# A decoder trunk on one core: the entry, the exit and the aftermath of a seven-product up projection

## The chip, the core and the metric

The kernel runs on one core of a Trainium2 chip. The core has five engines that matter here: TensorE (PE), which multiplies; VectorE (DVE); ScalarE (ACT); GpSimd (POOL); and SyncE (SP), which only issues DMAs. Each engine works through its own list of instructions in order and waits on semaphores. ACT issues DMAs as well, from within its own list. The metric is the device time of one execution in microseconds (us), as the median of several runs.

## The reference

Two groups of rows, a prompt of 1024 rows and 8 samples of 8 rows, go through two layers with the same weights; together they are T = 1088 columns of a transposed activation. Each layer is a token mixer, a gated feed-forward part and a gated addition:

```python
for i in range(DEPTH):
    j = i // N_MIXERS
    xn = rms_norm(h, g_mix[i])
    if i % N_MIXERS == 0:
        mix, s = short_conv_mixer(xn, st_a[j], a_w_in[j], a_conv[j], a_w_out[j])
    else:
        mix, s = conformer_conv_mixer(xn, st_b[j], ...)
    h = h + mix
    h = h + swiglu_ffn(rms_norm(h, g_ffn[i]), ffn_w_gu[i], ffn_w_down[i])
    gate = jax.nn.sigmoid(rms_norm(h, g_ple[i]) @ ple_w_gate[i])
    h = h + gate * (p[i] @ ple_w_proj[i])
return rms_norm(h, g_final), ...
```

D_MODEL is 1024 (KD = 8 tiles of 128) and D_FF is 2816 (KF = 22 tiles). Everything is float32. The change concerns layer 0 only: the end of its mixer, its up projection `x @ w_gu` with `silu(g) * u`, and its down projection.

## The kernel before, in words

**Precision.** Every float32 operand is cut into a high part, which PE takes in its faster float32 format, and a low part (the rest). A product is three matmuls: high by high, high by low, low by high. The high part of a weight (`whi`) is a copy on ACT. The low part (`wlo`) is a subtraction on POOL, or, for later weights, a load of a low part that was computed ahead of time and stored in DRAM.

**Staging.** Computing those low parts ahead of time is called staging (`stage`, line 245). 110 weight units of 512 KB are staged in 220 halves: load a half into `sraw`, copy its high part to `shi` on ACT, subtract on POOL, store the result (`dlo`). `stage()` is called after every block or product; the code keeps a running estimate of PE's time (`nc.tensor.at`, from the class `Paced`) and does one step whenever that estimate has advanced by `STAGE_EVERY`. In a step, ACT issues the store of the half that POOL has finished, copies the next half and issues the load of a new one. Before a pool of `sraw` buffers can be closed, `stage_with` (line 276) finishes all that is in flight, one half after the other.

**The mixer (`mixer_a`, line 520; 0 to about 440 us).** Its last step is eight items of four blocks each; a block is nine matmuls (three chunks of the 1088 columns, three partial products). The loop runs over `MIX_J` = 0, 4, 1, 5, 2, 6, 3, 7. After each item `mixer_end` (line 568) adds the PSUM result to h on DVE, writes h to DRAM (`hd`), adds the squares for the norm (`norm_stat`, also on DVE) and, after every second item, calls `operands(k)` (line 584) for the pair of row tiles k and k + 4. At its first item `at_end[0]` (`last_down`, line 1157) closes the staging's buffers, at its last item `at_end[1]` (`last_item`, line 1176) makes the first weights of the next stage ahead of the add.

**The seven-product stage (`ffn0_up`, line 631; about 420 to 906 us).** Each pair of gate and up weight tiles is multiplied as a 2 by 2 block product with seven instead of eight block multiplications. The seven products of a pair f are A11·B11, S2·T2, S3·T3, S1·T1, S4·B22, A12·B21 and A22·T4. The left factors are sums of quarter weights: `pair_fetch` loads a pair's raw weights on SP, `pair_sums` makes S1 to S4 on DVE, `pair_cell` cuts one of them into high and low parts in a ring of ten buffers. The right factors come from `operands`: B11, B21, B22 are halves of h times the gain, T1 to T4 are their differences. A product is 24 matmuls of 272 columns. `next_weights(m)` prepares pair f + 1 between the products of pair f. Within the first pair (f == 0) the sums of squares are reduced over the partitions by matmuls with a matrix of ones, and 1/sqrt is taken (`rms`, line 494): `rms[0]` cuts the sums into high and low parts, `rms[1]` does the matmuls and the root. At the end of each pair the activation is written to DRAM (`ad`). PSUM holds four buffers in this stage.

**The down projection (`ffn0_down`, line 695; from 932 us on).** h was given up for space and is loaded again from `hd`. The activations are loaded from `ad` into `ta`, cut into high (ACT) and low (DVE) parts, and multiplied in batches of `DOWN_0` = 3, 4, 4, 4, 4, 3. Each batch runs over the eight row tiles j; after each item DVE adds the PSUM result to h. The activations of the next batch are loaded and cut in the first items of this one. PSUM holds two buffers here. In the last batch, after its first item, `swap` (line 1217) does all staging that is left, closes the pools of the operands and opens those of the next stage; from then on each item is followed by two norm splits (`hna`, `hn`) on ACT and DVE.

**What sets the order.** The schedule is written by hand: the order of the calls is the order on each engine. SP's list holds the loads of weights, h and ta and the stores of h and ad; ACT's list holds the staging's DMAs.

Of the kernel before, what the change touches and what calls it, by code (L numbers as in the profile page):

```python
# [19 lines left out]
P = 128  # L20
# [42 lines left out]
DOWN_0 = [3, 4, 4, 4, 4, 3]  # L63
# [81 lines left out]
class Net:  # L145
# [3 lines left out]
    def __init__(self, ctx, tc, xT, wall, pT, sa, sb, vecs, yT, sa_p, sa_s, sb_p, sb_s):  # L149
# [16 lines left out]
        self.stage_slots, self.stage_at = None, 0.0  # L166
# [78 lines left out]
    def stage(self, flush=False):  # L245
# [23 lines left out]
        if self.to_stage and not flush:  # L269
            u, i = self.to_stage.popleft()  # L270
            raw = self.stage_slots[1]("sraw", F32)
            self.stage_slots.append(self.stage_slots.pop(1))
# [3 lines left out]
    def stage_with(self, slots):  # L276

        while self.stage_raw or self.staging:
            self.stage(True)
        self.stage_slots, self.stage_at = slots, self.nc.tensor.at  # L280

    def stage_tiles(self, pool, n):
        return [lambda name, dtype, i=i: pool.tile([P, WH], dtype, name=name, tag=f"s{i}", bufs=1) for i in range(n)]
# [236 lines left out]
    def mixer_a(self, y):  # L520
# [6 lines left out]
        def up(f):  # L527
# [6 lines left out]
            else:  # L534
                psc, psh = self.item(g, y), self.item(g, y)
            t = self.tmp(g)
# [31 lines left out]
    def mixer_end(self, i, ps):  # L568
# [15 lines left out]
    def operands(self, k):  # L584
# [14 lines left out]
        put("B21", hb[:, lo], gb)  # L599
        nc.scalar.activation(yb, hb, AF.Copy, scale=gb)  # L600
        nc.vector.tensor_tensor(ya[:, lo], ya[:, up], ya[:, lo], ALU.subtract)
        nc.vector.tensor_tensor(ya[:, up], yb[:, up], ya[:, up], ALU.subtract)
        put("T1", ya[:, lo])
        nc.vector.tensor_tensor(yb[:, up], yb[:, up], ya[:, lo], ALU.subtract)
        put("T2", yb[:, up])
        put("B22", hb[:, up], gb)
        put("T3", ya[:, up])
        nc.vector.tensor_tensor(yb[:, lo], yb[:, lo], yb[:, up], ALU.subtract)
# [853 lines left out]
```

## Time and profile before

| | us |
|---|---|
| runs before | 2595.93, 2598.44, 2743.23 |
| median | 2598.44 |
| profiled execution, its own time | 2593.68 |
| its span, first to last instruction | 2591.9 |
| PE busy | 2476.4 |
| DVE, ACT, POOL busy | 1403.2, 1001.4, 952.3 |

A profile row of the timeline gives the start, the length (us), the engine, the line, the operation with the names of what it writes and reads, its shape and its count; a bracket at the end gives the idle time of that engine just before and what ended it. All instructions of this kernel carry line 128, the helper that records them, so that rows are told apart by their tile names: `ps` is PSUM, `y` an operand of the seven products, `ya` and `yb` its sources, `w` and `ws` their weights and sums, `act` the down projection's operand, `hna` and `hn` the norm splits. A row of the waits gives the engine and what it writes, the engine and tile that it waited for, the total in us, the number of times and the longest. SPq and ACTq mark the issue of a DMA, not its transfer.

### The profile page before, as it was taken

The page shows a single profiled execution, that of the slowest core. Times are in us where ns is not written, and L with a number is a line of the kernel's source. Part 1 is how long each engine was busy: PE and PEld are TensorE (multiplying, and loading weights), DVE is VectorE, ACT ScalarE, POOL GpSimd, SP SyncE. Part 2 cuts the span into 40 slices and gives each one's busy share as a digit, 9 for nine tenths or more (in the row PEclk, how much of TensorE's full clock was granted, in tenths as well). Part 3 has the DMA queues.
Part 4 walks back from the last instruction along what each step waited for, and adds up shares of the span by engine and source line. Part 5 has one row for each costly group of instructions (what it writes and reads, how often), then busy time and mean ns, then how long its engine had stood idle before and what let it go on. Part 6 is the DMA issues. An engine that isn't in the chain of part 4 may idle for free.

```text
span 2591.9 us, 39114 instructions
## 1 busy us (share of the span) xinstructions
PE 2476.4 (96%) x15590; PEld 2283.1 (88%) x15590; DVE 1403.2 (54%) x1947; ACT 1001.4 (39%) x1377; POOL 952.3 (37%) x655
## 2 busy tenths in 40 slices
PE   9999987999999959995999999999999999999998
PEld 8898977999999949995789897888887899999997
DVE  5222238888888733333587776688865532222235
ACT  5222235433333323224554535444335542222235
POOL 3555551555555435554233433333333110000012
PEclk9999998999999979997999999999999999999999
DMA  4444442555555466554555475555555575454445
GB/s 139 138 154 157 141 140 97 181 188 193 189 185 191 153 244 213 199 197 138 181 195 197 167 190 177 188 186 189 188 188 193 186 259 202 167 163 163 164 163 198
DMA packets 183575, 462.71 MB, mean 179 GB/s; under 512 B 38368, under 2 KB 41824, under 8 KB 183392
## 3 DMA queue, kind: packets, MB, share of 16 engines
q1 hardware_dynamic: 118880, 342.60, 38.9%
q10 hardware_dynamic: 64512, 117.60, 14.1%
q8 instruction: 123, 2.02, 0.3%
q14 instruction: 60, 0.49, 0.1%
HBM read 375.65 MB, written 84.48 MB: 178 GB/s over the span
## 4 chain that ended last, share of the span: by engine, by line
PE 50%; DVE 2%; ACT 1%; DMA 1%; POOL 0%; issue 0%; ACTq 0%; DVEq 0%; POOLq 0%; SPq 0%
PE ps L128 50%; DMA dlo<-sraw 0%; POOL sraw L128 0%; DVE t L128 0%; DMA wlo<-dlo 0%; DVE acc L128 0%; DVE h L128 0%; ACT ua L128 0%; DVE hna L128 0%; DVE nt L128 0%; ACT cact L128 0%; ACT shi L128 0%; ACTq L128 0%; DMA sraw<-wall 0%; DVE nv L128 0%
## 5 line engine op out<-in xcount | busy, mean ns | idle before, releaser
L128 PE MATMUL ps<-hn,whi 128*128 128x288 f32 (+3 forms) x4416 | 915.1, 323 | 3.2 <-ACT whi L128 2.3
L128 PEld LDWEIGHTS ps<-hn,whi 128*128 128x128 f32 x4416 | 692.7, 189 | 58.5 <-ACT whi L128 2.5
L128 PE MATMUL ps<-act,whi 128*128 128x288 f32 (+1 forms) x2496 | 519.5, 332 | 74.5 <-DVE h L128 47.1
L128 PE MATMUL ps<-hn,wlo 128*128 128x288 f32 (+3 forms) x2208 | 562.8, 323 | 2.6 <-DMA wlo<-dlo 2.6
L128 PEld LDWEIGHTS ps<-act,whi 128*128 128x128 f32 x2496 | 392.9, 191 | 115.6 <-DVE h L128 37.2
L128 PE MATMUL ps<-y,w 128*128 128x272 f32 x3696 | 472.3, 290 | 11.6 <-ACT w L128 3.4
L128 PEld LDWEIGHTS ps<-y,w 128*128 128x128 f32 x3696 | 470.9, 190 | 13.1 <-ACT w L128 3.8
L128 POOL TENSOR_TENSOR sraw<-sraw,shi 128x512 fp32r<-128x512 f32 x220 | 318.6, 1448 | 359.8 <-issue 131.7
L128 PEld LDWEIGHTS ps<-hn,wlo 128*128 128x128 f32 x2208 | 364.8, 189 | 29.6 <-DMA wlo<-dlo 2.9
L128 ACT ACTIVATE whi<-wraw 128x1024 fp32r<-128x1024 f32 (+1 forms) x282 | 293.5, 1042 | 204.0 <-PE ps L128 158.5
L128 PE MATMUL ps<-act,wlo 128*128 128x288 f32 (+1 forms) x1248 | 306.8, 332 | 0.3 <-POOL wlo L128 0.3
L128 DVE TENSOR_TENSOR h<-ps,h 128x1088 f32<-128x1088 f32 (+2 forms) x200 | 184.7, 925 | 225.3 <-PE ps L128 225.0
L128 POOL TENSOR_TENSOR t<-t,r 128x512 f32<-128x512 f32 (+2 forms) x52 | 80.4, 1546 | 538.2 <-ACT t L128 493.1
L128 ACT ACTIVATE shi<-sraw 128x512 fp32r<-128x512 f32 x220 | 137.6, 625 | 300.6 <-POOL sraw L128 285.6
L128 DVE TENSOR_TENSOR t<-ps,t 128x544 f32<-128x544 f32 (+3 forms) x155 | 115.4, 746 | 255.4 <-PE ps L128 247.8
L128 PEld LDWEIGHTS ps<-act,wlo 128*128 128x128 f32 x1248 | 201.2, 191 | 19.6 <-POOL wlo L128 0.8
L128 ACT ACTIVATE t<-t 128x512 f32<-128x512 f32 (+5 forms) x107 | 76.6, 717 | 333.8 <-DVE t L128 333.7
L128 POOL TENSOR_TENSOR sqacc<-sqacc,sq 128x512 f32<-128x512 f32 (+4 forms) x69 | 97.7, 1416 | 261.8 <-ACT sq L128 261.5
L128 POOL TENSOR_TENSOR prod<-prod 128x512 f32<-128x512 f32 x96 | 124.2, 1303 | 180.7 <-ACT prod L128 180.6
L128 POOL TENSOR_TENSOR wlo<-wraw,whi 128x1024 fp32r<-128x1024 f32 (+1 forms) x54 | 136.1, 2524 | 138.2 <-ACT whi L128 132.3
L128 DVE TENSOR_TENSOR t<-ps,r 128x512 f32<-128x512 f32 (+3 forms) x116 | 78.9, 683 | 187.7 <-PE ps L128 186.9
L128 DVE SCALAR_TENSOR_TENSOR acc<-ub,vecs_sb,acc 128x512 f32<-128x512 f32 x184 | 137.6, 749 | 4.0 <-ACT acc L128 4.0
(154 smaller groups left out, 2419.6 us busy)
## 6 DMA issues: line engine op xcount, KB each, us to landing
wraw<-wall SPq DMA_DIRECT2D x322, 512.0 KB, 3.9
wlo<-dlo SPq DMA_DIRECT2D x226, 512.0 KB, 3.6
sraw<-wall ACTq DMA_DIRECT2D x220, 256.0 KB, 3.3
dlo<-sraw ACTq DMA_DIRECT2D x220, 256.0 KB, 2.5
ad<-t SPq DMA_DIRECT2D x22, 544.0 KB, 4.3
ta<-ad SPq DMA_DIRECT2D x22, 544.0 KB, 5.4
h<-xT SPq DMA_DIRECT2D x8, 544.0 KB, 6.8
hd<-h SPq DMA_DIRECT2D x8, 544.0 KB, 2.9
```

Source lines behind the costliest of these rows:

```text
L128: return f(out, *args, **kw)
```

## The change

- **Staging.** The buffers for `shi` and `sraw` are separate lists now (two and four in the mixer and in the down projection, one and four in the seven-product stage). A step is done every 3.9 instead of 4.4 counted us, from 30 instead of 50 on, with less catching up after a delay. A flag `stage_ends` stops the fetching of new halves while the steps go on. It is set in the mixer's last up item, at the start of the last pair of the seven-product stage, and in the fifth batch of the down projection at j = 5. `swap` does no staging any more and asserts that nothing is left to stage.
- **Operands in two parts.** `operands(k)` makes B11, B21 and the first difference, and leaves the rest (T2, T3, T1, B22, T4, in this order) to a function that the next `mixer_end` calls after its add of h. For the last pair it is called at once, ahead of the norm sum.
- **Norm sums.** In the first pair of the seven-product stage the cut of the sums moves behind the S2 product's add, and the matmuls with the ones matrix and the root move behind the S1 product.
- **Next weights.** For f > 0 each step of `next_weights` comes one product later.
- **The down projection's loads.** A function `early`, called in the last pair ahead of the S4 product, fetches the first two weight units, loads and cuts the first two activations and loads all eight tiles of h, in the order 3, 7, 1, 2, 4, 5, 0, 6. Before, this came after the last pair. The batches are 2, 4, 4, 4, 4, 4. Within the batches an activation is loaded from ACT's queue ahead of the item and cut after the item's add of h; before, SP's queue loaded it and it was cut at once, behind the add.

```diff
-DOWN_0 = [3, 4, 4, 4, 4, 3]
+DOWN_0 = [2, 4, 4, 4, 4, 4]
...
-        self.stage_at = max(self.stage_at + self.STAGE_EVERY, nc.tensor.at - 2 * self.STAGE_EVERY)
+        self.stage_at = max(self.stage_at + self.STAGE_EVERY, nc.tensor.at - self.STAGE_EVERY / 2)
         done, self.staging = self.staging, None
         nc.scalar.wait(nc.tensor)
-        ahead = len(self.stage_slots) - 3
+        his, raws = self.stage_slots
...
-        ready = len(self.stage_raw) == ahead or flush or not self.to_stage
-        if ready and self.stage_raw:
+        fetch = self.to_stage and not self.stage_ends
+        if self.stage_raw and (len(self.stage_raw) == len(raws) - 2 or not fetch):
             u, raw = self.stage_raw.popleft()
-            hi = self.stage_slots[0]("shi", F32R)
+            hi = his[0]("shi", F32R)
+            his.rotate(-1)
...
-        if self.to_stage and not flush:
+        if fetch:
...
                 psc, psh = self.item(g, y), self.item(g, y)
+                self.stage_ends = f == KD - 1
...
         self.add_h(g, j, ps)
+        if self.rest:
+            self.rest.pop()()
         self.hd[j] = self.pd.tile([P, T], F32, name=f"hd{j}")
         self.nc.sync.dma_start(self.hd[j], self.h[j])
         if i % 2:
             self.operands(j - KH)
+        if i == KD - 1:
+            self.rest.pop()()
         self.norm_stat(g, j, self.nc.vector)
...
+        nc.vector.tensor_tensor(ya[:, lo], ya[:, up], ya[:, lo], ALU.subtract)
         nc.scalar.activation(yb, hb, AF.Copy, scale=gb)
...
+        def rest():
+            nc.vector.tensor_tensor(ya[:, up], yb[:, up], ya[:, up], ALU.subtract)
+            nc.vector.tensor_tensor(yb[:, up], yb[:, up], ya[:, lo], ALU.subtract)
+            put("T2", yb[:, up])
+            put("T3", ya[:, up])
+            nc.vector.tensor_tensor(yb[:, lo], yb[:, lo], yb[:, up], ALU.subtract)
+            put("T1", ya[:, lo])
+            put("B22", hb[:, up], gb)
+            put("T4", yb[:, lo])
+
+        self.rest.append(rest)
...
-                if f == 0:
-                    m -= 2
+                m -= 1 if f else 2
...
             if f == 0:
-                rms[1]()
+                halves()
             next_weights(1)
             add(s[:, lo], go("S3", "T3"), t[:, up])
             next_weights(2)
             q = go("S1", "T1")
+            if f == 0:
+                factors()
             add(t[:, up], q, t[:, up])
             add(s[:, up], q, s[:, lo])
             next_weights(3)
+            if f == KF - 1:
+                early()
             add(t[:, up], go("S4", "B22"), t[:, up])
...
+    def act_load(self, queue):
+        f = len(self.acts)
+        low, high = (pool.tile([P, T], F32R, name="act", tag=tag, bufs=1) for pool, tag in self.places.popleft())
+        t = self.tmp(GJ, "ta")
+        queue.dma_start(t, self.ad[f])
+        self.acts.append((high, low))
+        return t
+
+    def act_split(self, f, t):
+        high, low = self.acts[f]
+        self.nc.scalar.activation(high, t, AF.Copy)
+        self.nc.vector.tensor_tensor(low, t, high.bitcast(F32), ALU.subtract)
...
             for j in range(KD):
-                self.add_h(g, j, self.item(g, acts[at:at + n]))
+                if not last and j < DOWN_0[b + 1]:
+                    loads.append((len(self.acts), self.act_load(nc.scalar)))
+                if b == len(DOWN_0) - 2 and j == KD - 3:
+                    self.stage_ends = True
+                self.add_h(g, j, self.item(g, self.acts[at:at + n]))
+                if loads:
+                    self.act_split(*loads.pop(0))
...
+        def early():
+
+            self.n_raw = self.n_prep = N_MIX + 2 * KF
+            self.blk = self.n_raw * KD
+            self.limit = len(self.order)
+            self.n_conv += 2
+            self.fetch_to(self.n_raw + self.RAW)
+            t = [self.act_load(nc.sync) for _ in range(DOWN_0[0])]
+            self.prep_to(self.n_raw - self.RAW + 1)
+            for f in range(DOWN_0[0]):
+                self.act_split(f, t[f])
+            for j in range(KD):
+                self.h[j] = ph.tile([P, T], F32, name=f"h{j}", tag=f"h{j}")
+            for j in 3, 7, 1, 2, 4, 5, 0, 6:
+                nc.sync.dma_start(self.h[j], self.hd[j])
...
         def swap():
-            for _ in range(len(self.to_stage)):
-                self.stage_at = 0.0
-                self.stage()
-            self.stage_with(None)
+            assert not self.to_stage
+            self.stage_with()
...
-    STAGE_EVERY = 4.4
-    STAGE_FROM = 50.0
+    STAGE_EVERY = 3.9
+    STAGE_FROM = 30.0
```

More of the change, by code (lines that the diff above doesn't have):

```diff
@@ L268, in stage, with stage_with, stage_tiles @@
             self.staging = u, raw
-        if self.to_stage and not flush:
+        if fetch:
             u, i = self.to_stage.popleft()
-            raw = self.stage_slots[1]("sraw", F32)
-            self.stage_slots.append(self.stage_slots.pop(1))
+            raw = raws[0]("sraw", F32)
+            raws.rotate(-1)
             nc.scalar.dma_start(raw, self.wall[u][:, i * WH:(i + 1) * WH])
             self.stage_raw.append(((u, i), raw))
-    def stage_with(self, slots):
+    def stage_with(self, his=None, raws=None):
+        self.stage_ends = True
         while self.stage_raw or self.staging:
             self.stage(True)
-        self.stage_slots, self.stage_at = slots, self.nc.tensor.at
-    def stage_tiles(self, pool, n):
-        return [lambda name, dtype, i=i: pool.tile([P, WH], dtype, name=name, tag=f"s{i}", bufs=1) for i in range(n)]
+        self.stage_slots, self.stage_at = his and (deque(his), deque(raws)), self.nc.tensor.at
+        self.stage_ends = False
+    def stage_tiles(self, pool, a, b):
+        return [lambda name, dtype, i=i: pool.tile([P, WH], dtype, name=name, tag=f"s{i}", bufs=1) for i in range(a, b)]
     ORDER = "A11", "S2", "S3", "S1", "S4", "A12", "A22"
@@ L635, in ffn0_up, with halves @@
         r = self.rg(g)
-        rms = [f for _, f in self.rms(g, 0, 0)]
+        self.parts = [self.pt.tile([P, T], F32R, name=n, tag="t") for n in ("sh", "sl")]
+        def halves():
+            nc.scalar.activation(self.parts[0], self.sqacc, AF.Copy)
+            nc.vector.tensor_tensor(self.parts[1], self.sqacc, self.parts[0].bitcast(F32), ALU.subtract)
+        (_, _), (_, factors) = self.rms(g, 0, 0)
         for f in range(KF):
             if f == 0:
-                rms[0]()
                 self.pair_fetch(1)
+            if f == KF - 1:
+                self.stage_ends = True
             t, s = self.tmp(g), self.tmp(g, "s")
@@ L1137, in run @@
         self.pu0 = pool("u0", c_u, bufs=2)
-        self.hd, self.ad, self.right = {}, {}, {}
-        self.stage_with(self.stage_tiles(pool("stage_m", c_st), 6))
+        self.hd, self.ad, self.right, self.rest = {}, {}, {}, []
+        p = pool("stage_m", c_st)
+        self.stage_with(self.stage_tiles(p, 0, 2), self.stage_tiles(p, 2, 6))
         self.stage_at = self.STAGE_FROM
@@ L1191, in run @@
         self.PSW = GS.width
-        self.stage_with(self.stage_tiles(pool("stage_u", c_st), 5))
-        self.ffn0_up()
-        self.stage_with(None)
+        p = pool("stage_u", c_st)
+        self.stage_with(self.stage_tiles(p, 0, 1), self.stage_tiles(p, 1, 5))
+        py, py2 = self.cells["T2", 0][0], self.cells["B11", 0][0]
+        places = [[(py2, f"z{2 * i}"), (py2, f"z{2 * i + 1}")] for i in range(3)]
+        places += [[(py, f"y{2 * i}"), (py, f"y{2 * i + 1}")] for i in range(5)]
+        self.places = deque(places[i % len(places)] for i in range(KF - DOWN_0[-1]))
+        self.acts = []
+        def early():
[12 more added lines that the diff above has]
+                nc.sync.dma_start(self.h[j], self.hd[j])
+        self.ffn0_up(early)
+        self.stage_with()
         c_st.close()
-        self.n_conv += 2
         c_x.close()
@@ L1226, in swap @@
             self.pYA = pool("y_a", c_ya, side="right", bufs=KD)
-        ya, yb = self.ffn0_down(places, swap)
+        ya, yb = self.ffn0_down(swap)
         c_x.close()
```

53 lines of the change are left out of this document (12 added, 41 removed).

## The prediction, made before the changed kernel ran

> **What bounds the kernel now.** I read the page first, then the waits of the whole run, then TensorE (PE) alone by windows, then the timeline around each hole.
>
> ```profile
> span 2591.9 us, 39114 instructions
> PE 2476.4 (96%) x15590; PEld 2283.1 (88%) x15590; DVE 1403.2 (54%) x1947; ACT 1001.4 (39%) x1377; POOL 952.3 (37%) x655
> PE   9999987999999959995999999999999999999998
> ```
>
> PE sets the time: 115.5 us of the span are idle, and the slices show three holes in the first half (slices 7, 15 and 19). The waits name them:
>
> ```profile
> PE ps L128 <- DVE h L128: 47.1, 6, 27.2
> PE ps L128 <- ACT whi L128: 28.5, 2, 26.2
> ```
>
> They are the stage's entry (about 353 to 481 us), its exit (906 to 957) and the place where the down projection changes its pools (1180 to 1213). A hole costs more than its idle time; PE by windows (length, busy, granted clock):
>
> ```profile
> 353.30:481.00 127.70, 100.62 (x612) 0.87 0.33 114
> 402.70:407.30 4.60, 4.58 (x18) 0.63 0.38 148
> 932.30:935.90 3.60, 3.29 (x10) 0.50 0.13 11
> 951.90:956.60 4.70, 4.66 (x19) 0.64 0.32 74
> 1207.60:1213.00 5.40, 5.30 (x19) 0.54 0.15 42
> ```
>
> Behind each hole PE runs at half to two thirds of its clock: 1.7, 1.8, 1.7 and 2.5 us lost (length times the missing clock).
>
> **The pool change (third hole).**
>
> ```profile
> 1178.40:1204.30 25.90, 6.29 (x10) 12.62 (x10) 0.63 0.61 203
> 1171.61 1.29 DVE L128 TENSOR_TENSOR h<-ps,h 128x1088 f32<-128x1088 f32 x1 [3.16 <-PE ps L128]
> 1204.20 0.72 ACT L128 ACTIVATE hna<-h,vecs_sb 128x512 fp32r<-128x512 f32 x1 [1.80 <-POOL sraw L128]
> 1206.36 1.28 DVE L128 TENSOR_TENSOR h<-ps,h 128x1088 f32<-128x1088 f32 x1
> 1207.69 2.18 PE L128 MATMUL ps<-act,whi 128*128 128x288 f32 x6 [27.24 <-DVE h L128]
> 1214.45 1.16 PE L128 MATMUL ps<-act,whi 128*128 128x288 f32 x6
> 1215.95 1.16 PE L128 MATMUL ps<-act,whi 128*128 128x288 f32 x6
> ```
>
> The first row holds ACT's and POOL's work on shi: ten weight halves are still staged at 2.5 us each, one after the other, ahead of the hna copy on ACT. DVE waits for hna, the next add of h stands behind it, and PE has only two PSUM buffers. Cost: 27.24 + 2.5 = 29.7 us.
>
> The change empties this work earlier. A block of nine matmuls takes 1.50 us (last two rows), for which the pacing counts 1.39, so one half per 3.9 counted is one per 4.2 us. Until the mark (fifth batch, j = 5) there are about 300 us of the mixer (from counted 30 to its own mark near 341), 147 products of 3.02 us (444 us; 21.1 us for seven is in the exit's first row) and 132 blocks (198 us): 942 / 4.2 = 224 halves, and 220 are wanted. From the mark to the swap 16 blocks follow, 24 us, nearly six steps, for the three still in flight. So the swap finds nothing to flush. I take 28.5 of the 29.7; bounds 22 (three halves left) and 29.7. The faster staging lies beside PE: POOL is busy 37% and ACT 39%, and neither made PE wait in a steady stretch.
>
> **The exit (second hole).**
>
> ```profile
> 884.83 21.32 PE L128 MATMUL ps<-y,w 128*128 128x272 f32 x168
> 888.84 21.45 SPq L693 DMA_DIRECT2D ad<-t  x2
> 910.34 7.14 SPq L1206 DMA_DIRECT2D h<-hd  x8
> 932.34 2.18 PE L128 MATMUL ps<-act,whi 128*128 128x288 f32 x6 [26.19 <-ACT whi L128]
> 948.25 1.11 ACT L128 ACTIVATE act<-ta 128x1088 fp32r<-128x1088 f32 x1 [7.50 <-DMA ta<-ad]
> 951.94 1.26 PE L128 MATMUL ps<-act,whi 128*128 128x288 f32 x6 [3.91 <-DVE h L128]
> DMA to landing us min/median/max: 4.3/5.4/9.3
> ```
>
> Before, SP issues h, then ta, then the weights only after the last pair's store. Lost: 26.19 + 1.8, then 3.91 + 1.7, and 0.6 of small waits: 34.2 us.
>
> After, two weight units, two ta tiles and h go out within the last pair. Counting from the last pair's start (884.8), with landings of 4.5 to 5.5 us (last row): SP issues the store of pair 20 at 889 and is free, the raws land by 895, the ta tiles by 896 and 898.5 (the second waits for that store to give back its buffer), and the two splits (1.11 on ACT, on DVE as long as an add of h, 1.28 each) end at 901, while the S4 product ends at 899.9 (five of 3.02). They stand ahead of the S4 add on DVE; that add is 1 us late, which free PSUM buffers cover. SP's h loads queue behind the third raw (which waits for wlo) and, for h5, h0, h6, behind the products that last read those slots; h0 lands near 910, just when DVE gets to the first add. So PE restarts about 1 us after the last product.
>
> What is late next is the first batch. It has two activations now, so an item lasts 3 us, and in its first four items one activation each is loaded through **ACT's queue**: trigger, landing, copy, and only then the next trigger. With 4.5 us to land (minimum 4.3 for one alone) and 1.11 + 0.35, a step takes 6 us. DVE's subtract waits for it, and the next add of h stands behind the subtract, so with two PSUM buffers PE follows the 6 us steps: items 4, 5 and 6 wait 1.9, 2.9 and 2.8, and one slow restart adds 1.7. In the later batches an item lasts 6 us and the step hides. Left: 1 + 7.6 + 1.7 and about 1 for staging steps between, 11.3; gain **23 us**. Bounds: 13 (steps of 8.5 us: the median landing plus two staging copies) and 30 (all hidden but the restart).
>
> The Trainium skill (DMA: Bandwidth & Descriptors, the cost of one DMA) gives a fixed 2.0 us and bytes over 436 GB/s, an estimate of 3.3 us for these 557 KB; no load here landed in less than 4.3, and by the rule the batch would wait some 3 us less, 2528 in all.
>
> **The entry (first hole).**
>
> ```profile
> 365.44 1.29 DVE L128 TENSOR_TENSOR h<-ps,h 128x1088 f32<-128x1088 f32 x1 [4.79 <-PE ps L128]
> 373.76 0.78 DVE L128 SCALAR_TENSOR_TENSOR y<-h,vecs_sb,y 128x544 fp32r<-128x544 f32 x1 [7.04 <-ACT y L128]
> 386.91 2.15 PE L128 MATMUL ps<-act,whi 128*128 128x288 f32 x6 [9.35 <-DVE h L128]
> 389.15 1.28 DVE L128 TENSOR_TENSOR h<-ps,h 128x1088 f32<-128x1088 f32 x1
> 401.29 1.28 DVE L128 TENSOR_TENSOR h<-ps,h 128x1088 f32<-128x1088 f32 x1
> 402.72 1.43 PE L128 MATMUL ps<-act,whi 128*128 128x288 f32 x6 [2.22 <-DVE h L128]
> 404.96 1.28 DVE L128 TENSOR_TENSOR h<-ps,h 128x1088 f32<-128x1088 f32 x1
> 420.71 1.75 DVE L128 TENSOR_TENSOR ws<-wraw 128x512 f32<-128x512 f32 x1
> 428.05 1.28 DVE L128 TENSOR_TENSOR h<-ps,h 128x1088 f32<-128x1088 f32 x1
> 430.08 8.69 PE L128 MATMUL ps<-y,w 128*128 128x272 f32 x52 [0.81 <-DVE y L128]
> 444.47 28.90 PE L128 MATMUL ps<-y,w 128*128 128x272 f32 x216
> 473.21 0.69 DVE L128 TENSOR_TENSOR ws<-wraw 128x512 f32<-128x512 f32 x1 [6.17 <-DMA wraw<-wall]
> 476.65 23.56 PE L128 MATMUL ps<-y,w 128*128 128x272 f32 x185 [3.28 <-DVE t L128]
> ```
>
> A flush of staging on ACT holds the first operands back 7.04 us; from there DVE is the bound until 444. Two items cost it 15.8 us (389.15 to 404.96), PE 12. Without the flush the chain starts at 366.7. With the operands in two parts the second part goes to the even item, and T2, T3, T1 are copied back to back, so most of DVE's waits for ACT's copies go; I count 5.5 us for an odd and 8.6 for an even item (1.21 per add, 0.65 per half-width operation): 14.1. The even item of step 2 starts with PE at 371.4, so the chain reaches the pair-0 sums at 408.2 (420.71 before), the last add of h at 415.5 (7.3 us of sums and cells, as before) and the first operand B11 of the last k at 417.6 against 430.1: 12.5 us earlier.
>
> The norm sums now follow S1, so five products run on without them. They need PE 14.8 us with a slow start, the sums 1.5, and DVE's three reads come after the pair-1 sums, at 434.3; S4 starts at 434.9. Before it was 444.47 + 1.7 + two products, 452.2. PE's 3.28 wait for the pair-2 raws' sums comes again (raws at 459, adds at 462). Gain **16 us**. Bounds: 7 (the flush alone; also what is left if S4 had to wait for S1's own buffer through the whole 1/sqrt chain, which it does not if the buffer given back first goes out first), and 22 (no second wait).
>
> The Trainium skill (TensorE: Matmul & The Clock Gate, the two clock states) has the clock fall after a whole idle window of about 3.4 us. Here 2.22 us of waiting were enough for 0.63, but 16 us after a longer hole. By the rule the short waits of the first down batch would keep the clock and give 1.7 us back; by the row they do not.
>
> **Edits that I cost at nothing.** *The earlier end of fetching* in the mixer and in the last pair: three halves in flight need 12.6 us, and 12 blocks (18 us) or seven products (21 us) follow the mark. If that cover were gone, each half left would cost ACT 2.5 us, as in the third hole. *The second shi buffer* takes away a wait of ACT for POOL that no PE wait hung on. *The batches of 2 and 4 instead of 3 and 3* hold the same 176 blocks; the last batch's items grow from 4.5 to 6 us, above what ACT and DVE do in one (add, two copies, two subtracts). *The act loads on ACT* leave SP to the weights, which it held up before (a load at ACT's head waits for no weight buffer); in exchange ACT's weight copies stand behind a landing, up to 6 us late, under units of 12 us prepared two ahead.
>
> **The sum.** 28.5 + 23 + 16 = 67.5 us. The profiled execution took 2593.7 us around its 2591.9 us span, and would take 2526; the median of the runs is 2598.4, so I forecast **2531 us**.
>
> **Rivals.**
> *Load chain.* The first down batch goes at 9 us per step, since ACT's staging triggers wait for POOL behind wlo. For it: two wlo fall in that time. Against: staging restarts with two steps that only fetch. Four steps of 3 us more: 2543.
> *Entry stays DVE's.* Splitting saves no time on DVE, only the flush goes: 9 us less, 2540. For it: DVE's number of operations is the same. Against: 3 us of waits per two items.
> *Not dry.* The margin of 4 in 224 is thin; if four halves are flushed at the swap, 10 us and a slow restart come back: 2543. This is how the change would not do what it says.
> *Slower.* The next pair's weights are made one product later, and their fetch now stands behind the Silu:
>
> ```profile
> 728.93 3.28 SPq L295 DMA_DIRECT2D wraw<-wall  x2
> 735.97 1.12 ACT L128 ACTIVATE t<-t 128x1088 f32<-128x1088 f32 x1 [7.17 <-DVE t L128]
> 740.61 0.68 DVE L128 TENSOR_TENSOR ws<-wraw 128x512 f32<-128x512 f32 x1
> ```
>
> The second raw is issued near 732 and wanted at 740.6. After, copy and subtract follow the Silu (ends 737.1), the fetch goes near 741 and lands near 745.5, and DVE wants it after the S2 add at 743.7: 2 us of waiting, which DVE's idle time in a pair (21.1 us less some 17 of work) covers. From a landing of about 6.6 us on (the 2 us of waiting grown to the 4.1 us that DVE is idle in a pair), DVE falls behind in each pair and PE waits. At 2.5 us and a slow restart of 1.7, 20 pairs cost 84 us: 2615.
>
> **Chances and range.** Forecast 0.60, load chain 0.14, entry 0.12, not dry 0.06, slower 0.05, something unseen 0.03. The lower bounds of the three terms sum to 42 us, the upper to 82: 2556 and 2517; I give **2515 to 2558**, which holds the first three rivals. 2% (2546.5), about what a measurement of this kernel can tell from no change, lies inside: of the forecast most and of the three near rivals half are beyond it, so faster 0.72; same 0.25; slower 0.03, the far end of the last rival.
>
> **What would show it.** Right: no shi copy between the fifth down batch and the first hna; PE's gap there under 2 us; PE's gap after the last product under 3 us, then waits of 2 to 3 us for h in the first batch; B11 of the last k near 418 us; the norm-sum matmuls after the fifth product. Wrong: a wait for DVE or DMA that returns once per pair; more than 40 us of PE idle time in the first 1250 us beside these; PE's total idle time above 75 us.

## The result, and the profile after

| | before | after |
|---|---|---|
| median of the runs, us | 2597.18 (2592.58 to 2743.23) | 2553.21 (2551.33 to 2554.08) |
| ratio, 95% interval | | 0.9836 (0.9816 to 0.9855) |
| profiled execution, span | 2591.9 | 2552.3 |
| PE busy, idle in the span | 2476.4, 115.5 | 2479.3, 73.0 |

The 2743 us run of before was disturbed and is not in the ratio. The change makes the kernel 1.6% faster, 43 us against the median of the other three runs (2595.93); forecast were 67.5 us and 2531. The time lies inside the stated range (2515 to 2558), near its slow end, and the gain is short of the 2% that had been given a chance of 0.72. The page of the kernel after, the head and the line of slices:

```profile
span 2552.3 us, 39083 instructions
PE 2479.3 (97%) x15590; PEld 2285.3 (90%) x15590; DVE 1409.4 (55%) x1947; ACT 1003.1 (39%) x1377; POOL 952.3 (37%) x655
PE   9899988999999989999999999999999999999997
```

Of the three holes of before (slices 7, 15 and 19) the last is gone and the others read 8, but slice 2, in the mixer, is a new one. The third hole first, as the group of the staging's copies between 900 and 1250 us:

```profile
L128 ACT ACTIVATE shi<-sraw x45: 612/632/636, 901.8 to 1115.5; 128x512 fp32r<-128x512 f32 x45
```

The last copy to shi starts at 1115.5, 35 us ahead of the first hna copy (1150.3), and PE does not wait between 950 and 1250 us. The exit, from the timeline of SP, PE and DVE:

```profile
910.73 0.33 SPq L193 DMA_DIRECT2D wraw<-wall  x1
911.12 6.76 SPq L1238 DMA_DIRECT2D h<-hd  x8
917.37 1.17 PE L128 MATMUL ps<-act,whi 128*128 128x288 f32 x6
928.28 1.29 DVE L128 TENSOR_TENSOR h<-ps,h 128x1088 f32<-128x1088 f32 x1 [5.13 <-DMA h<-hd]
929.62 2.18 PE L128 MATMUL ps<-act,whi 128*128 128x288 f32 x6 [6.14 <-DVE h L128]
942.33 1.26 PE L128 MATMUL ps<-act,whi 128*128 128x288 f32 x6 [1.26 <-DVE h L128]
945.97 1.25 PE L128 MATMUL ps<-act,whi 128*128 128x288 f32 x6 [0.40 <-DVE h L128]
```

PE goes from the last product into the first down batch with no gap (917.37), then stands 6.14 us for h0, whose load SP issued after 911.12. The entry, from the timeline of PE:

```profile
440.88 0.82 PE L128 MATMUL ps<-y,w 128*128 128x272 f32 x2 [2.21 <-ACT y L128]
442.51 14.61 PE L128 MATMUL ps<-y,w 128*128 128x272 f32 x100 [0.81 <-DVE y L128]
456.95 0.29 PE L128 MATMUL ps<-sh,ones_r 128*128 128x288 f32 x1
458.67 24.78 PE L128 MATMUL ps<-y,w 128*128 128x272 f32 x192 [0.58 <-DVE sqacc L128]
487.83 2.41 PE L128 MATMUL ps<-y,w 128*128 128x272 f32 x9 [4.37 <-DVE s L128]
```

The first operand of the last k (442.51) and S4 (458.67) come within 1 us of the forecast times, 417.6 and 434.9, plus 24.7: everything here is late already. The loss lies ahead of it, in the mixer, where the forecast had none. PE's timeline there:

```profile
79.80 2.18 PE L128 MATMUL ps<-hn,whi 128*128 128x288 f32 x6 [8.31 <-ACT t L128]
139.20 2.11 PE L128 MATMUL ps<-act,whi 128*128 128x288 f32 x6 [3.31 <-DVE h L128]
219.90 1.27 PE L128 MATMUL ps<-hn,whi 128*128 128x288 f32 x6 [1.52 <-ACT t L128]
241.33 1.89 PE L128 MATMUL ps<-act,whi 128*128 128x288 f32 x6 [3.33 <-DVE h L128]
325.38 2.18 PE L128 MATMUL ps<-hn,whi 128*128 128x288 f32 x6 [4.66 <-ACT t L128]
```

And PE by windows behind each of these waits (start and end, length, busy, granted clock; the last two columns, DMA share and GB/s, are not used here):

```profile
79.80:84.70 4.90, 4.90 (x16) 0.50 0.23 73
139.20:143.40 4.20, 4.20 (x16) 0.59 0.58 182
219.90:222.50 2.60, 2.60 (x16) 1.00 0.21 79
241.30:245.20 3.90, 3.87 (x14) 0.56 0.45 152
325.40:330.00 4.60, 4.60 (x15) 0.50 0.16 51
```

These waits and two small ones at the end (1.40 and 0.56) make 23.1 us; before, the mixer had 0.68, 3.68 and 0.55, 4.9 us. The slow stretches lose 8.2 us (length times the missing clock), before 1.7. Together 18.2 + 6.5 = 24.7 us.

**A measure for all that follows.** Every kernel here issues the same 15,590 matmuls, in the same order but for the six of the norm sums. So the start of matmul number k, minus its start in the profiled run of before, is what was lost (+) or won (-) up to that place. Matmul 2100 is near the start of the mixer's last step, 2800 behind the entry, 5900 near the end of the product stage, 6200 behind the exit, 7500 behind the pool change, 15589 the last.

| kernel (us against before) | 600 | 900 | 1500 | 2100 | 2800 | 5900 | 6200 | 7500 | 15589 |
|---|---|---|---|---|---|---|---|---|---|
| after | +10.5 | +14.4 | +15.8 | +24.7 | +9.5 | +11.4 | -12.3 | -41.6 | -40.4 |
| e1 before with the new pace | +7.7 | +13.1 | +16.2 | +27.6 | +28.9 | +28.9 | +28.8 | -0.6 | +2.4 |
| e2 after, mixer's old pace | -1.0 | +2.4 | +3.5 | +3.5 | -9.6 | -0.5 | -21.8 | -50.8 | -48.3 |
| e3 after, copy first | -0.6 | +12.6 | +16.8 | +23.8 | +9.8 | +12.5 | -11.4 | -40.8 | -39.4 |
| e4 before, no staging in the mixer | -0.9 | -2.1 | -7.9 | -8.8 | -16.9 | -16.9 | -17.1 | +136.0 | +152.0 |
| e5 after, store issued by POOL | +10.8 | +17.4 | +22.6 | +29.8 | +16.0 | +17.9 | -6.4 | -35.8 | -33.2 |
| e6 e2, flush back | -0.8 | +2.5 | +3.6 | +3.6 | -3.4 | +0.2 | -21.8 | -51.2 | -51.0 |
| e7 e2, operands in one part | -0.8 | +1.9 | +3.7 | +3.7 | -7.3 | +1.2 | -19.5 | -48.9 | -47.3 |
| e8 e2, norm sums back | -0.5 | +3.4 | +4.4 | +4.5 | -9.3 | -2.8 | -23.7 | -53.1 | -51.4 |
| e9 after, u by r on DVE | +11.7 | +15.3 | +14.7 | +20.2 | +6.4 | +7.9 | -17.9 | -47.3 | -45.3 |
| e10 after, from 50 us | -0.4 | +6.8 | +8.3 | +16.7 | +2.1 | +6.1 | -18.3 | -48.0 | -46.1 |
| e11 old pace, h0 first | -0.3 | -0.3 | +1.0 | +1.1 | -12.7 | -10.5 | -35.2 | -64.6 | -65.2 |
| e12 after, raw stored | +5.1 | +5.8 | +6.8 | +9.8 | -5.7 | -5.7 | -29.7 | -59.4 | -57.6 |

The kernel after by its differences: mixer +24.7, entry -13.3 (24.7 to 11.4; it is at 9.5 by matmul 2800, and 1.9 us are lost again by 3500), exit -23.7, pool change -29.3, the rest +1.2.

### The profile page after: what moved, and what is told of

It is laid out like the page before. It is cut to its first block, busy times and chain, and to the rows that moved or that the text cites. A ratio compares the mean times of both kernels' runs of the same rounds, so it can differ in the third digit from the quotient of the medians.

```text
span 2552.3 us, 39083 instructions
## 1 busy us (share of the span) xinstructions
PE 2479.3 (97%) x15590; PEld 2285.3 (90%) x15590; DVE 1409.4 (55%) x1947; ACT 1003.1 (39%) x1377; POOL 952.3 (37%) x655
## 4 chain that ended last, share of the span: by engine, by line
PE 73%; DVE 2%; DMA 2%; ACT 1%; issue 1%; POOL 0%; DVEq 0%; ACTq 0%; SPq 0%; POOLq 0%
PE ps L128 73%; DMA ta<-ad 1%; DVE t L128 1%; DVE h L128 0%; DMA wlo<-dlo 0%; DMA sraw<-wall 0%; DVE acc L128 0%; DVE hna L128 0%; ACT act L128 0%; DVE nt L128 0%; ACT ua L128 0%; DVE w L128 0%; DMA ad<-t 0%; POOL sraw L128 0%; ACT cact L128 0%
## 5 line engine op out<-in xcount | busy, mean ns | idle before, releaser
L128 PE MATMUL ps<-act,whi 128*128 128x288 f32 (+1 forms) x2496 | 516.4, 331 | 17.3 <-DVE h L128 14.7
L128 PEld LDWEIGHTS ps<-act,whi 128*128 128x128 f32 x2496 | 390.5, 190 | 57.9 <-DVE h L128 16.7
L128 POOL TENSOR_TENSOR sraw<-sraw,shi 128x512 fp32r<-128x512 f32 x220 | 323.8, 1472 | 214.3 <-ACT shi L128 95.5
L128 POOL TENSOR_TENSOR w<-wraw,w 128x512 fp32r<-128x512 f32 x66 | 99.9, 1514 | 123.6 <-ACT w L128 123.5
```

Source lines behind the costliest of these rows:

```text
L128: return f(out, *args, **kw)
```

## The experiments

**What makes the mixer wait: the theory.** In an up item ACT stood ahead of its copy of ps into t like this, first after, then before (ACT's timeline):

```profile
60.38 1.11 ACT L128 ACTIVATE act<-t 128x1088 fp32r<-128x1088 f32 x1 [6.74 <-DVE t L128]
...
66.74 0.63 ACT L128 ACTIVATE shi<-sraw 128x512 fp32r<-128x512 f32 x1 [3.77 <-POOL sraw L128]
69.20 0.63 ACT L128 ACTIVATE shi<-sraw 128x512 fp32r<-128x512 f32 x1 [1.83 <-POOL sraw L128]
...
75.54 0.63 ACT L128 ACTIVATE shi<-sraw 128x512 fp32r<-128x512 f32 x1 [3.25 <-POOL sraw L128]
78.03 0.63 ACT L128 ACTIVATE shi<-sraw 128x512 fp32r<-128x512 f32 x1 [1.86 <-POOL sraw L128]
78.67 1.08 ACT L128 ACTIVATE t<-ps 128x1088 f32<-128x1088 f32 x1
```

```profile
60.63 1.11 ACT L128 ACTIVATE act<-t 128x1088 fp32r<-128x1088 f32 x1 [6.73 <-DVE t L128]
...
63.55 1.06 ACT L128 ACTIVATE t<-ps 128x1088 f32<-128x1088 f32 x1
```

The copy gives PE a PSUM buffer back, and it comes 15 us later. Between stand staging steps, each a serial round: copy on ACT, subtract on POOL, and only then ACT may issue the store and go on, 2.5 us a round (66.74 to 69.20, 75.54 to 78.03). A round is longer where POOL first makes the low part of another weight: two such subtractions (2.49 us at 62.58, 2.34 us at 71.20 on POOL) stand in the rounds 62.35 to 66.74 and 71.66 to 75.54, 4.4 and 3.9 us.

### e1: the pace alone, in the kernel before

```diff
-    STAGE_EVERY = 4.4
-    STAGE_FROM = 50.0
+    STAGE_EVERY = 3.9
+    STAGE_FROM = 30.0
```

> The kernel before with the two constants of the faster staging alone (a step every 3.9 us instead of 4.4, from 30 us instead of 50). Theory A (in the mixer's up part each staging step is a serial round of ScalarE and GpSimd of about 2.5 us ahead of the copy that frees the PSUM buffer, and at 3.9 us these rounds no longer fit): TensorE's matmul number 2100 comes 12 to 25 us later than in the kernel before, with waits for ScalarE's copy of ps. Theory B (the new lists of slots, two for the high halves and four for the raw ones, make the wait): it comes within 4 us of the kernel before. Theory C (only the earlier start at 30 us does it): about 10 us later by matmul 600, nothing added behind that. Behind the mixer the third hole should shrink, since fewer halves are left to flush there.

2596.93 us beside 2598.46 for before, one run. Two numbers in the kernel before cost the mixer 27.6 us, somewhat more than the 12 to 25 that theory A gave, with the old lists of slots (one buffer for the high half, five for the raw ones): theory B falls. The loss does not stop at matmul 600 (+7.7), so theory C falls too. The third hole closes (+28.8 to -0.6), and that pays the mixer back and no more: alone, this part of the change is worth nothing that one run can show.

### e2: the mixer's old pace in the kernel after

```diff
-        self.stage_at = max(self.stage_at + self.STAGE_EVERY, nc.tensor.at - self.STAGE_EVERY / 2)
+        self.stage_at = max(self.stage_at + self.STAGE_EVERY, nc.tensor.at - self.STAGE_BACK)
...
+        self.STAGE_EVERY, self.STAGE_BACK = 3.4, 1.7
         p = pool("stage_u", c_st)
...
-    STAGE_EVERY = 3.9
-    STAGE_FROM = 30.0
+    STAGE_EVERY = 4.4
+    STAGE_BACK = 8.8
+    STAGE_FROM = 50.0
```

> The changed kernel with the mixer's staging as it was (a step every 4.4 us from 50 us on, with its old room to catch up of 8.8 us), and a step every 3.4 us in the product stage and the down part so that the list is empty before the pools change. Theory A: the mixer's loss of 24.7 us goes (matmul 2100 within 4 us of the kernel before), the rest stays as in the changed kernel: about 2530 us. Theory B: the loss stays at 20 to 25 us, 2553 us. If the faster steps in the product stage or the down part cost what they cost in the mixer, the total is above 2540 although the mixer's loss is gone.

2546.44 us (2544.26 to 2547.34), ratio 0.9797 (0.9783 to 0.9812). The mixer's loss is gone (+3.5), as theory A has it. But the time is 16 us above the 2530 that this alone would give: between 2800 and 5900 the gain runs out from -9.6 to -0.5. PE's waits in the product stage:

```profile
PE ps L128 <- DVE s L128: 7.9, 4, 5.7
PE ps L128 <- DVE t L128: 4.8, 8, 1.8
```

The 5.7 us one belongs to the entry (the kernel after has it too, 4.37); the other eleven, 7.0 us with slow restarts between, are scattered over the stage: at 3.4 us per step the product stage pays too, as the last sentence of the expectation feared. At 3.9 it pays little: 1.9 us in the kernel after (+9.5 to +11.4), and 2.2 in e11 (-12.7 to -10.5), which has e2's mixer and 3.9 us here, against 9.1 in e2.

### e3: the copy ahead of the second product, in the kernel after

```diff
-                psc, psh = self.item(g, y), self.item(g, y)
-                self.stage_ends = f == KD - 1
+                psc = self.item(g, y)
             t = self.tmp(g)
             nc.scalar.activation(t, psc, AF.Copy)
+            if f:
+                psh = self.item(g, y)
+                self.stage_ends = f == KD - 1
```

> The changed kernel with one line moved: the mixer's up part issues ScalarE's copy of the first product's PSUM buffer before the second product instead of behind it, so that at most half as many staging steps stand ahead of it on ScalarE; the pace stays at 3.9 us from 30 us. Theory A: the waits of 8.31, 1.52 and 4.66 us for that copy shrink below 2 us together and their slow restarts with them, the two waits of 3.3 us for VectorE's step may stay: matmul 2100 comes 5 to 10 us later than in the kernel before instead of 24.7, total about 2535 to 2540 us. If the place of the copy in ScalarE's order isn't what matters, the time stays near 2553 us.

2556.85 us (2555.09 to 2561.14), ratio 0.9844 (0.9828 to 0.9861): no better than the kernel after, and the 5 to 10 us that theory A gave for the mixer were missed (23.8). The waits for the t copy are gone, as expected, and the first one with them (-0.6 at 600), but others stand in their place. PE's waits up to 420 us:

```profile
PE ps L128 <- DVE h L128: 12.7, 3, 6.8
PE ps L128 <- ACT act L128: 5.7, 1, 5.7
PE ps L128 <- DVE t L128: 4.5, 1, 4.5
```

So it isn't one badly placed instruction. It looks as if ACT were short of time over the whole up item, and whatever is needed next from it late; that this also lies behind the two waits for DVE was not tested.

### e4: no staging in the mixer of the kernel before

```diff
-    STAGE_FROM = 50.0
+    STAGE_FROM = 1000.0
```

> The kernel before with no staging in the mixer at all (the first step is due at 1000 us by the planner's clock, the stages behind it start at once as before). Some 75 more halves are then flushed one by one when the pools change, so the total grows by 150 to 250 us, and only the mixer is read. Theory A: matmul 2100 comes 2 to 7 us earlier than in the kernel before, and the waits for PSUM buffers in the up part (0.68 and 3.68 us) are gone: staging sets all of the idle time there. If other work sets it, these waits stay and matmul 2100 comes within 1 us of the kernel before.

2746.48 us, one run, with the flush of the remaining halves behind it. The mixer is 8.8 us faster than in before, 2 us more than I expected, and PE has no wait from the start to 370 us. All idle time of the up part in the kernel before is staging's. Measured against this run, staging costs 8.8 us in the mixer of before and, by difference, 33.5 (24.7 + 8.8) in that of after.

### e5: the store issued by GpSimd, in the kernel after

```diff
             nc.gpsimd.tensor_tensor(raw.bitcast(F32R), raw, hi.bitcast(F32), ALU.subtract)
-            self.staging = u, raw
+            (v, i), q = u, nc.gpsimd
+            if v not in self.staged:
+                self.staged[v] = self.pd.tile([P, KD * P], F32, name=f"dlo{v}")
+            q.dma_start(self.staged[v][:, i * WH:(i + 1) * WH], raw)
```

> The changed kernel, its pace of 3.9 us from 30 us kept, but the store of each finished low half is issued by GpSimd itself, right behind its subtract, instead of by ScalarE one step later. ScalarE then has nothing to wait for in a staging step but its own copy. The first four runs put the mixer's loss down to the pace, whatever the lists of slots and the place of the copy. Theory A in its sharper form (ScalarE, in order, stands 156 us of the mixer's 390 waiting for GpSimd's subtract before it may issue that store, and the faster pace adds nine such waits): the loss of 24.7 us at matmul 2100 falls below 10 us, and the waits of TensorE for ScalarE's copies go. Rival: GpSimd itself, or the number of instructions on ScalarE, is what runs out at 3.9 us: the loss stays above 15 us. GpSimd's issuing may cost something of its own everywhere; the place to read is the mixer.

2561.61 us, one run; the mixer loses 29.8 us instead of 24.7. My expectation was wrong. POOL's timeline shows why:

```profile
103.32 1.30 POOL L128 TENSOR_TENSOR sraw<-sraw,shi 128x512 fp32r<-128x512 f32 x1
105.03 0.56 POOL L128 DMA_DIRECT2D dlo<-sraw  x1 [0.41 <-POOL sraw L128]
105.61 1.31 POOL L128 TENSOR_TENSOR sraw<-sraw,shi 128x512 fp32r<-128x512 f32 x1
```

On POOL the subtract, the wait for its end and the issue follow one another, 2.3 us per step (103.32 to 105.61). The round moved to another engine and kept its length, so the loss stayed. ACT's waiting for POOL's sraw did fall, from 155.8 to 62.4 us (30 to 420 us); in its place came 42.6 us of waits for the stores (DMA dlo<-sraw), ahead of loads that ACT still issues. So ACT's waiting for POOL is not by itself the measure of the loss.

### e6, e7, e8: the entry, one part undone at a time

Each is the kernel of e2 with one part taken back. e6:

```diff
                 psc, psh = self.item(g, y), self.item(g, y)
-                self.stage_ends = f == KD - 1
```

> The kernel of run e2 (changed kernel with the mixer's old pace) with the flag that ends the mixer's fetching taken out, so that the last halves are flushed when the staging's buffers are closed, at the mixer's first output item. Prediction's step: the flush held VectorE's first operand back 7.0 us and all behind it, so the entry (matmul 2100 to 2600) is about 7 us longer than in e2. Rival: VectorE has room by the last items, or the waits behind swallow it: under 3 us.

2543.36 us, one run. At matmul 2256 e2 stands at -7.7 and this one at -0.6: 7.1 us, the forecast's 7.04. At 2800 it is still 6.2 us behind. Then e2's fast staging swallows the difference (0.7 us at 5900), so its total shows none of it.

e7:

```diff
         self.add_h(g, j, ps)
-        if self.rest:
-            self.rest.pop()()
...
-        if i == KD - 1:
-            self.rest.pop()()
...
-        self.rest.append(rest)
+        rest()
```

> The kernel of run e2 with each pair's operands made at once again (in the changed order of copies, without the second part being left to the next item). Prediction's step: two parts save VectorE 1.7 us per two items, some 5 us until the first operand of the last k, so the entry is 3 to 6 us longer than in e2. Rival (the split saves no time on VectorE, whose number of operations is the same): within 1.5 us.

2547.25 us, one run. At matmul 2328, the last items, 4.6 us are lost against e2 (-6.6 and -11.2), where the forecast had 5.5; at 2800 2.3 us remain.

e8:

```diff
             if f == 0:
+                halves()
                 self.pair_fetch(1)
...
             if f == 0:
-                halves()
+                factors()
             next_weights(1)
...
             q = go("S1", "T1")
-            if f == 0:
-                factors()
```

> The kernel of run e2 with the norm sums cut ahead of the first product and multiplied behind the second, as before the change. Prediction's step: their two waits of 2.6 and 0.7 us and a slow restart come back ahead of the third product, about 5 us longer than in e2 by matmul 2600, of which the later wait for the next pair's sums may give some back. Rival: that later wait (5.7 us in e2, for VectorE's s) takes up all of it, and matmul 2600 is within 1.5 us of e2.

2543.22 us, one run. At matmul 2470, behind the norm sums of both kernels, it stands 4.3 us behind e2 (-9.5 and -13.8), at 2600 3.9 and at 2800 0.3 us. The rival's mechanism holds, one stage later than it said: in e2 PE reaches the second pair earlier, and waits there for the next pair's sums instead, 5.67 us against 1.97 in e8. In both kernels DVE can start those sums only when the raw weights land, at 465.14 and 465.39. In the kernel after the wait is 4.37 us, before 3.28. On the kernel of e2 the move of the norm sums brings nothing.

### e9: u by r on VectorE, in the kernel after

```diff
-                nc.gpsimd.tensor_tensor(o, o, i, ALU.mult)
+                nc.vector.tensor_tensor(o, o, i, ALU.mult)
```

> The changed kernel, pace of 3.9 us from 30 us kept, with GpSimd's two multiplications of u by r in each up item of the mixer done by VectorE instead. The run before it (e5) has refuted that ScalarE's own wait ahead of the store is what costs: with the store on GpSimd's queue the mixer lost 29.8 us. Theory A in its last form (ScalarE and GpSimd hand a half to and fro in rounds of 2.5 us; an up item of about 37 us at the pace of 3.9 has 9.4 such rounds, 24 us, beside the weights' low parts of 2.4 us each and the item's own chain, in which u by r takes GpSimd 2.3 to 3 us and some 6 us of standing for VectorE, so the two engines together have no room left): with u off GpSimd the loss at matmul 2100 falls from 24.7 to below 12 us. Rival (the raw buffers: a load waits for the store of its slot, and the ring of four turns no faster): the loss stays above 18 us.

2549.5 us, one run; the mixer loses 20.2 us. By my own numbers that speaks for the rival. ACT's timeline shows what the run left as it was:

```profile
112.14 0.63 ACT L128 ACTIVATE shi<-sraw 128x512 fp32r<-128x512 f32 x1 [3.20 <-POOL sraw L128]
114.65 0.63 ACT L128 ACTIVATE shi<-sraw 128x512 fp32r<-128x512 f32 x1 [1.88 <-POOL sraw L128]
115.40 1.08 ACT L128 ACTIVATE t<-ps 128x1088 f32<-128x1088 f32 x1
```

The rounds of 2.5 us ahead of the copy are as long as ever. POOL's work on u was not what made them long.

### e10: the kernel after, its pace without the earlier start

```diff
+        self.STAGE_EVERY = 3.3
         self.stage_with(at[:2], at[2:])
...
-    STAGE_FROM = 30.0
+    STAGE_FROM = 50.0
```

> The changed kernel with the staging's start at 50 us again, the pace of 3.9 us kept in the mixer and the product stage, and 3.3 us in the down part so that the list is empty in time. If the earlier start makes only the first wait (8.31 us and its slow restart, 10.5 us of the 24.7 at matmul 600) and the pace the others: about 0 at matmul 600 and 10 to 17 us later at matmul 2100. If the start makes all of it: within 4 us. If the pace alone does: 20 us or more. In the down part, at 3.3 us per step, no new wait of TensorE (within 1.5 us of the changed kernel from matmul 6200 to 7450).

2548.15 us, one run: -0.4 at matmul 600 and +16.7 at 2100, within the first forecast. An up item of 24 blocks takes 36 us; at 4.4 counted (4.75 us) that is 7.6 steps, at 3.9 (4.2 us) 8.6. One more round of 2.5 us in each of seven up items would be 17.5 us, an estimate that holds if ACT has no room left. The remaining 8 us are the start's. In the down part a step every 3.3 us costs nothing (-18.3 at 6200, -48.0 behind the pool change).

### e11: the version that the runs point to

With the lines of e2 for the mixer's pace, and:

```diff
+        self.STAGE_EVERY, self.STAGE_BACK = 3.9, 1.95
         p = pool("stage_u", c_st)
...
+        self.STAGE_EVERY, self.STAGE_BACK = 3.3, 1.65
         self.stage_with(at[:2], at[2:])
...
-            for n, j in ("B21", 0), ("T1", 4), ("T2", 1), ("B22", 5), ("T3", 2), ("T4", 6):
+            for n, j in ("B21", 5), ("T1", 2), ("T2", 0), ("B22", 4), ("T3", 1), ("T4", 6):
...
-            for j in 3, 7, 1, 2, 4, 5, 0, 6:
+            for j in 0, 1, 2, 3, 4, 7, 5, 6:
```

> The changed kernel with what the runs point to: the mixer's old pace (4.4 us from 50 us, catching up by 8.8), the product stage at 3.9 as changed, the down part at 3.3 so that the list is empty in time, and h0 loaded first: the last pair's operands sit in other tiles of h (T2 in h0, T3 in h1, T1 in h2, B22 in h4, B21 in h5, T4 in h6), so that h0 to h2 are given back first, and h is loaded in the order 0, 1, 2, 3, 4, 7, 5, 6. The mixer's loss goes (21 us less than the changed kernel at matmul 2100), the wait of 6.14 us for h0 and the 1.3 and 0.4 us behind it go with their slow restart (about 8 us), the third hole stays closed: 2523 to 2534 us, faster than the kernel before by 2.5 to 2.9% and than the changed kernel by 0.8 to 1.2%. If h's landings are late for another reason than the order and the slots, the 6 us stay: 2531 to 2540.

2529.55 us (2527.93 to 2535.04), ratio to before 0.9742 (0.9728 to 0.9755): faster than both kernels. The total is as expected, the exit is not: it wins 24.7 us (-10.5 to -35.2), only 1.0 more than after. PE's timeline there, and its windows (length, busy, clock) behind the first two waits:

```profile
907.22 2.18 PE L128 MATMUL ps<-act,whi 128*128 128x288 f32 x6 [2.63 <-DVE h L128]
914.86 1.23 PE L128 MATMUL ps<-act,whi 128*128 128x288 f32 x6 [3.01 <-DVE h L128]
918.75 1.26 PE L128 MATMUL ps<-act,whi 128*128 128x288 f32 x6 [0.67 <-DVE h L128]
923.04 1.26 PE L128 MATMUL ps<-act,whi 128*128 128x288 f32 x6 [1.05 <-DVE h L128]
```

```profile
907.20:911.20 4.00, 3.98 (x16) 0.61 0.99 403
914.80:917.00 2.20, 2.14 (x13) 1.00 0.46 115
```

h0 is in time, and four other waits appear, 7.4 us together: the chain of act loads through ACT's queue that the prediction described (7.6 us in three waits). ACT's copies start at 903.53, 911.08, 915.06 and 919.35, each once its load has landed, so the steps are 7.6, 4.0 and 4.3 us, not 6 each. In the kernel after most of this chain lay behind the wait for h0.

### e12: the raw half stored, in the kernel after

```diff
-            nc.gpsimd.tensor_tensor(raw.bitcast(F32R), raw, hi.bitcast(F32), ALU.subtract)
+            nc.gpsimd.tensor_tensor(hi, raw, hi.bitcast(F32), ALU.subtract)
```

> The changed kernel, pace of 3.9 us from 30 us kept, every instruction of the staging kept, but GpSimd's subtract writes into the high half's buffer and the raw half is stored as it was loaded: the later low parts are thus left out of the result. ScalarE's store no longer has to wait for GpSimd, and its next copy only for the subtract two steps back. The two runs before that tried theory A (e5, e9) took nothing away that counts: with the store on GpSimd's queue a step took GpSimd 2.3 us instead, and without u by r the rounds stayed. Theory A (ScalarE and GpSimd passing one half to and fro, 2.5 us a step, is the price of a step in the mixer): the loss of 24.7 us at matmul 2100 falls below 10 us, and ScalarE's waiting for GpSimd's sraw there from 156 to below 80 us. Rival (GpSimd's own time, the ring of raw buffers or the DMAs set the price): these are unchanged, and the loss stays above 15 us.

2536.7 us, one run. This kernel leaves the low parts of the staged weights out of what it stores, so its result is not the reference's; all instructions are there, only the hand-over is gone. The mixer's loss falls to 9.8 us. ACT's waits from 30 to 420 us, after and then e12:

```profile
ACT shi L128 <- POOL sraw L128: 155.8, 48, 7.9
```

```profile
ACT shi L128 <- POOL shi L128: 47.2, 13, 6.9
ACT shi L128 <- DMA sraw<-wall: 35.1, 19, 9.5
```

The waiting for POOL falls from 155.8 to 47.2 us, and with it 15 of the 24.7 us go. Theory A holds for these: this much of the price is the round between two engines that work in order. What is left, 9.8 us, lies just under my bound; against no staging at all (e4, -8.8) it is 18.6 of 33.5 us, so more than half of what staging costs in this mixer is not shown to be the hand-over. Of the 9.8 us, 5.1 are there by matmul 600, which would fit the earlier start; whether the rest comes from ACT's 35 us of waiting for its own loads in the ring of four raw buffers was not tried. With the hand-over in place five raw buffers did not help: e1 has them and loses 27.6 us.

## Why the prediction was right or wrong, point by point

**The pool change, 28.5 us: right.** 29.3 measured, and no shi copy ran behind the mark. That the list would be empty in time was right as well.

**The step that failed: "The faster staging lies beside PE: POOL is busy 37% and ACT 39%, and neither made PE wait in a steady stretch."** I priced the faster staging at nothing, and it cost 24.7 us, nearly all of the miss: 67.5 us of gain were forecast, and by the last matmul there are 40.4. The three terms of the sum gave 66.3 us together (29.3, 23.7, 13.3); that the time still lies inside the range is luck, for the range was made from bounds of these terms and held nothing for the mixer. Three things were wrong in it. The shares are means over the whole run, and busy time leaves out the time in which ACT stands at the head of its list waiting for POOL; in the mixer of the kernel before (30 to 420 us) that alone was 139 us, more than the 126 us of its busy time there:

```profile
ACT shi L128 <- POOL sraw L128: 139.1, 39, 7.9
```

The 2.5 us per half that I quoted for the third hole was the price of a step everywhere that ACT runs behind, and I used it only there. And the mixer of before did have waits (0.68 and 3.68 us), which e4 shows to be staging's: the stretch was already full. A step more per up item, 2.5 us each, would have been the sum to make. The signs that I set were too coarse to ring: these waits are 23 us where 40 were asked for beside the three holes, PE's total idle time is 73.0 where 75 were, and a quarter of the loss is slow clock.

**The entry, 16 us: 13.3.** The flush was worth 7.1 of the forecast 7.0 (e6) and the two parts 4.6 of 5.5 (e7), both read where they act, in the kernel of e2. The term that gave nothing there is the norm sums, some 5 us by the forecast's own times: of the 3.9 us won ahead of the second wait, which the prediction took to stay near 3.3, that wait took 3.7 back (e8).

**The exit, 23 us: 23.7, the size right by luck and the path wrong.** PE restarted with no gap, better than the 1 us forecast. "h0 lands near 910, just when DVE gets to the first add" was wrong. The kernel after is 11.4 us later than before at this place, so that 910 stands for 921 here; but the third raw unit held SP until 910.73, h0 was seventh in the order, and DVE, free near 923, could add only at 928.28. The loads took longer too: the ta loads between 895 and 950 us landed in 3.6 to 8.9 us, median 7.6, where the prediction had 4.5 to 5.5. The chain of load steps was real but lay behind the wait for h0; e11 brought it to light with 2.63, 3.01, 0.67 and 1.05 us. One wait of 6.1 us had taken the place of the forecast 7.6.

**The rivals.** *Slower* did not happen: no wait returns once per pair, the product stage holds its shift from matmul 3500 to 5900 (+11.4). *Load chain* and *Entry stays DVE's* name real costs, but the time near theirs came from elsewhere. *Not dry* did not happen. The case that did, the mixer slowed by the staging itself, I had not named.

## What to carry to other kernels

Before work is moved under "idle" engines, count for the stretch itself how long those engines stand waiting at the head of their lists; a step that passes between two in-order engines can cost the first of them the whole round trip, here 2.5 us for a copy of 0.63. A wait that ends an item can hide a second chain of like length, so price the next one before promising the first one's full gain. And when time is won ahead of a wait for something that has its own clock (here a load of weights), the wait can grow by nearly all of it (3.7 of 3.9 us in e8).

## What the runs showed of the hardware that I had not expected

Whether a wait of two to three microseconds costs the clock does not follow from its length: after 2.63 us (e11, 907.22) the granted clock was 0.61, after a longer one of 3.01 (914.86) it was 1.00, after 1.52 (219.90, kernel after) 1.00, after 3.31 0.59. What decides is where the wait falls. In each of the 14 traces the granted clock changes only on a fixed grid of 3.41 us, and four periods of e11's grid, around its first two waits, show the rule (length, PE busy, clock):

```profile
903.47:906.88 3.41, 1.13 (x7) 1.00 0.97 364
906.88:910.29 3.41, 3.07 (x10) 0.50 1.02 418
910.29:913.70 3.41, 1.56 (x10) 1.00 0.73 241
913.70:917.12 3.42, 2.26 (x14) 1.00 0.59 187
```

The first wait leaves 2.28 us of one period idle, and the next period runs at half clock; the longer second wait is split over two periods, 1.85 and 1.16 us, and costs nothing. Over the 14 traces, by the profile's busy times of PE, every period at full clock with more than 1.87 us idle was followed by one at half clock, none with less than 1.52 us was, and the full clock came back only after a period with at most 0.65 us idle. A period at half clock loses 1.7 us, the slow restart of the prediction. The Trainium skill (TensorE: Matmul & The Clock Gate, What's actually happening) has the clock fall after a whole idle window of about 3.4 us and calls the window free-running; the grid agrees with the second part, while 2.28 us of idle time in a period of 3.41 is less than the first part asks for.

A DMA issue on POOL is not free either: 0.56 us, and 0.41 us of waiting for the subtract ahead of it (e5, 105.03).
